# A hybrid decoder layer on one core: the mixer's recurrence, taps and norm put in a fixed order, and the first stage's small changes

## The chip, the cores and the metric

One core of a Trainium2 chip runs the whole layer in one launch. The metric is device time in microseconds (us), the median of several executions. PE is TensorE's matmul, PEld its weight load, DVE VectorE, ACT ScalarE, POOL GpSimd, SP SyncE (which issues most transfers).

## The reference, cut to what matters

The layer works on 512 tokens of 1024 channels in float32. Two half-step feed-forward parts stand around a mixer; each part begins with an RMS norm.

```
x = x + 1/2 * FFN1(rmsnorm(x));  x = x + mixer(rmsnorm(x));  x = x + 1/2 * FFN2(rmsnorm(x));  y = rmsnorm(x)

z = h @ w_in                                   # 4 x 512 channels: c_val, c_gate, r_x, r_gate
u  = c_val * sigmoid(c_gate)
u  = silu(layernorm(depthwise_conv31(u)))      # the convolution's half
xr = depthwise_conv4(r_x)
r, i = sigmoid(blockdiag(xr, w_a)), sigmoid(blockdiag(xr, w_x))      # the two gates
a  = exp(-8 r softplus(-lam));  h_t = a_t h_(t-1) + sqrt(1 - a_t^2) (i_t xr_t)
yr = h * gelu(r_gate)                          # the recurrence's half
mixer = [u ; yr] @ w_out
```

## The kernel before, in words

Every float32 product is made of three products of two parts each, high times high, high times low and low times high. The parts are made on the chip: ACT rounds a tile to its high part, DVE subtracts that from the tile for the low part. In the feed-forward parts a block scheme of seven products is used (`mm_block`, L331); the mixer uses plain products over eight slices of the contraction (`mm_feat`, L316) and products by token tile (`mm_tok`, L557 to L559).

A Python list of `Unit`s is the order of PE's work. For each unit `run` traces its products, then lets generators (`chains`, `convs`, `pool_convs`) trace a step of the side work, and then traces the unit's evacuation. A planner afterwards orders the instructions of each engine by priority, which is the place where they were traced (moved by `tc.high_priority(offset)`), and by its own idea of when each is ready. `tc.keep_in_program_order(ins)`, called `pin` in places, ties an instruction behind the one that was traced just before it on its engine.

In the mixer the units come in this order: the convolution's gate and value for its four channel tiles of 128 (`zc_units`, tiles 0 and 1, then 2), the four tiles of the recurrence's input (`rx_units`), the convolution's tile 3, the four tiles of the recurrence's gate branch (`rg_units`), and the output products (`out_units`). The output products of the recurrence's half read `yhi` and `ylo` (four tiles c, in two pairs q); those of the convolution's half read `uhi` and `ulo`. Token tiles t are 0 to 3, output halves `oh` 0 and 1.

The side work: `conv_dve` makes a convolution tile on DVE, 31 multiply-adds (taps, L704 to L710) into two PSUM banks `pc` and one last addition (L714); tile 1 goes by ACT and POOL (`conv_pool`). `lru` is the recurrence: eight gate products `pga` on PE (L827), a sigmoid on ACT behind each (L828), two products on POOL (L833), tanh, exp and square on ACT (L837 to L842), one product for each pair on DVE (L845), square roots on ACT (L849), products on POOL (L850), then for each pair two scans over time (L859), the product with the GeLU branch `gl` (L864), the high part on ACT (L865) and the low part on DVE (L866). `layernorm` takes the mean by `channel_sum` on PE (`pm`, L677), subtracts it, squares, sums on PE again, takes the root on ACT (L750), the reciprocal on DVE (L763, in two halves of 256 tokens), then product (L767), SiLU (L768), high part (L769) and low part (L759).

In the first stage PE runs products of a constant tile (`keep_busy`, L954, counts in `IDLE`) between the first steps; `grow` is the first norm's weight row, spread over the partitions by two products with one row (L959).

Of the kernel before, what the change touches and what calls it, by code (L numbers as in the profile page):

```python
# [8 lines left out]
F32 = mybir.dt.float32  # L9
# [18 lines left out]
PLAIN = (3, 2)  # L28
BESIDE = (4, 5, 6, 9, 11, 13, 15, 18, 20)
ASIDE = 16  # L30
IDLE = (7, 3, 3, 3)
CUT = 128
TAPS = 31
PR_NORM = 800
# [4 lines left out]
PR_SIDE = -400  # L39
PR_OUT = 300  # L40
PR_COMB = 0
SCAN_LATER = 5
RMS_EPS = 1e-6
LN_EPS = 1e-5
A, B, ALL = (0, HT), (HT, HT), (0, T)
# [30 lines left out]
def layer_kernel(ctx: ExitStack, tc, x, gains, w_g1, w_u1, w_d1a, w_d1b, w_in,  # L76
# [47 lines left out]

    nc.sync.dma_start(xt[0], x[0:P, :])
    grow = sp.tile([1, D], F32, name="grow", tag="gbc", bufs=1)
    nc.sync.dma_start(grow, gains[0:1, :])
    nc.sync.dma_start(xt[1], x[P:2 * P, :])

    def load_gain(i):  # L130
# [9 lines left out]
    def dve(us):  # L140
        clock["dve"] = max(clock["dve"], clock["pe"] - 3.0) + us

    def step_chains():
        for c in list(chains):
            with tc.high_priority(offset=c[0]):
                if next(c[1], None) is None:
                    chains.remove(c)

    def step_convs():
        while convs and clock["dve"] < clock["pe"]:  # L150
            with tc.high_priority(offset=PR_CONV):
                us = next(convs[0], None)
            if us is None:
                convs.pop(0)
            else:
                dve(us)
        while pool_convs and clock["pool"] < clock["pe"]:
            clock["pool"] = max(clock["pool"], clock["pe"] - 3.0)
            with tc.high_priority(offset=PR_CONV):
                us = next(pool_convs[0], None)  # L160
            if us is None:
                pool_convs.pop(0)
            else:
                clock["pool"] += us
# [468 lines left out]
    def par(c, i):  # L633
        return ch[:, c, i:i + 1]

    def zc_units(c, parts):
        off = ASIDE if len(parts) == 2 else 0
        sgt, sv = Slab(split=ws_in[4 + c], off=off), Slab(split=ws_in[c], off=off)
        box = {}

        def product(key, s, t0, n):
            box[key] = bank("pz")
            mm_feat(box[key][:, :n], s, t0, n, CUT if key == "g" and c == 0 else 0)

        def gate_out(n):
            box["s"] = sp.tile([P, T], F32, name=nm("sgc"), tag="sg", bufs=2)
            S.activation(box["s"][:, :n], box["g"][:, :n], AF.Sigmoid)

        def val_out(t0, n):
            V.tensor_mul(mx["ub"][:, c, 30 + t0:30 + t0 + n], box["v"][:, :n], box["s"][:, :n])  # L650
            dve(0.7)
            if c != 1:
                convs.append(conv_dve(c, t0, n))
            elif t0 + n == T:
                pool_convs.append(conv_pool(c))
            if c == 3:
                chains.append((PR_LRU, lru()))

        out_ = []
        for t0, n in parts:  # L660
            us = 5.44 * n / 512
            out_.append(Unit([sgt], us, lambda t0=t0, n=n: product("g", sgt, t0, n),
                             lambda n=n: gate_out(n)))
            out_.append(Unit([sv], us, lambda t0=t0, n=n: product("v", sv, t0, n),
                             lambda t0=t0, n=n: val_out(t0, n)))
        return out_
# [14 lines left out]
    def conv_done(c):  # L681
        done["conv", c] = True
        if c < 3 and all(("conv", i) in done for i in range(3)):
            pm["s"] = slot([P, T], "cs")
            G.tensor_add(pm["s"], conv_out(0), conv_out(2))
            G.tensor_add(pm["s"], pm["s"], conv_out(1))
# [9 lines left out]
    def conv_dve(c, t0, n):  # L696
        if t0 == 0:
            accs[c] = [bank("pc"), bank("pc")]
        acc, o, at = accs[c], conv_out(c), slice(t0, t0 + n)
        us = 0.66 if n == T else 0.42  # L700
        for j in range(TAPS):
            src, to = mx["ub"][:, c, t0 + j:t0 + j + n], acc[j % 2][:, at]
            if j == 0:
                V.tensor_scalar(out=to, in0=src, scalar1=par(c, P_DW),  # L704
                                scalar2=par(c, P_DWB), op0=ALU.mult, op1=ALU.add)
            elif j == 1:
                V.tensor_scalar(out=to, in0=src, scalar1=par(c, P_DW + 1), scalar2=None,
                                op0=ALU.mult)
            else:
                V.scalar_tensor_tensor(out=o[:, at] if j == TAPS - 2 else to, in0=src,  # L710
                                       scalar=par(c, P_DW + j), in1=to,
                                       op0=ALU.mult, op1=ALU.add)
            yield us
        V.tensor_add(o[:, at], acc[0][:, at], o[:, at])  # L714
        yield us
        if t0 + n == T:
            conv_done(c)


    def conv_pool(c):  # L720
# [18 lines left out]
    def layernorm():  # L739
        mu = pm["mean"]  # L740
        sq = [slot([P, 2, T], "sq") for _ in range(2)]
        for c in range(4):
            v = conv_out(c)
            V.tensor_sub(v, v, mu)
            dve(0.69)
            S.activation(sq[c // 2][:, c % 2, :], v, AF.Square)
        yield 1
        var = channel_sum([sq[c // 2][:, c % 2, :] for c in range(4)])
        rs = sp.tile([P, T], F32, name=nm("rs"), tag="sg", bufs=2)
        S.activation(rs, var, AF.Sqrt, bias=lneps)  # L750
        done["var"] = True
        yield 1
        hi, lo = two("uhi", F32R), two("ulo", F32R)
        half = [slice(0, HT), slice(HT, T)]

        def low(sl):
            for c in range(4):
                v, o = conv_out(c)[:, sl], hi[c // 2][:, c % 2, sl]
                V.tensor_sub(lo[c // 2][:, c % 2, sl], v, o.bitcast(F32))  # L759
            dve(1.6)  # L760

        for i, sl in enumerate(half):
            V.reciprocal(rs[:, sl], rs[:, sl])  # L763
            dve(1.8)
            for c in range(4):
                v, o = conv_out(c)[:, sl], hi[c // 2][:, c % 2, sl]
                V.tensor_mul(v, v, rs[:, sl])  # L767
                S.activation(v, v, AF.Silu, scale=par(c, P_LNG), bias=par(c, P_LNB))  # L768
                S.copy(o, v)  # L769
            dve(1.6)  # L770
            if i:
                low(half[0])
        low(half[1])
        done["u"] = (hi, lo)

    lr = {}
# [41 lines left out]
            out_.append(Unit([s], 5.44, lambda c=c, s=s: product(c, s), lambda c=c: evac(c)))  # L818
        return out_

    def lru():
        xr, r, i_, th = lr["xr"], two("r"), two("i"), two("th")
        for c in range(4):
            at = (slice(None), c % 2, slice(None))
            for gi, (to, b) in enumerate(((r, P_BA), (i_, P_BX))):
                pga = bank("pga")
                PE.matmul(pga, bd[:, gi, c, :], xr[c // 2][at], start=True, stop=True)  # L827
                S.activation(to[c // 2][at], pga, AF.Sigmoid, bias=par(c, b))  # L828
            if c % 2:
                yield 1  # L830
        pin = tc.keep_in_program_order
        for q in range(2):
            G.tensor_mul(xr[q], xr[q], i_[q])  # L833
            clock["pool"] += 2.4
# [5 lines left out]
            pin(S.activation(r[c // 2][at], r[c // 2][at], AF.Exp, scale=nsp[:, c:c + 1]))  # L840
        for q in range(2):
            pin(S.activation(i_[q], r[q], AF.Square))  # L842
        yield 1
        for q in range(2):
            pin(V.scalar_tensor_tensor(out=th[q], in0=i_[q], scalar=1.0, in1=th[q],  # L845
                                       op0=ALU.add, op1=ALU.mult))
            dve(1.2)
        for q in range(2):
            S.activation(th[q], th[q], AF.Sqrt)  # L849
            G.tensor_mul(xr[q], xr[q], th[q])  # L850
            clock["pool"] += 2.4
        done["roots"] = True
        for _ in range(SCAN_LATER):
            yield 1
        hi, lo = two("yhi", F32R), two("ylo", F32R)
        for q in range(2):
            for c in (2 * q, 2 * q + 1):
                at = (slice(None), c % 2, slice(None))
                pin(V.tensor_tensor_scan(th[c // 2][at], r[c // 2][at], xr[c // 2][at],  # L859
                                         0.0, ALU.mult, ALU.add))  # L860
                dve(1.2)
            while ("gl", 2 * q + 1) not in done:
                yield 1
            pin(V.tensor_mul(th[q], th[q], lr["gl"][q]))  # L864
            S.copy(hi[q], th[q])  # L865
            V.tensor_sub(lo[q], th[q], hi[q].bitcast(F32))  # L866
            dve(2.4)
            done["y", q] = (hi, lo)


    def out_units(after):
# [31 lines left out]
        def fin_two():  # L903
            for t in range(2):
# [1 line left out]
                    fin(t, oh)  # L906

        out_ = [Unit(sy, 5.44, lambda: part((0, 1), sy, ("y", 0), True, (0, 1))),
                Unit(sy, 2.72, lambda: part((0,), sy, ("y", 1), True, (2, 3))),
                Unit([], 0.0, mean),  # L910
                Unit(sy, 2.72, lambda: part((1,), sy, ("y", 1), True, (2, 3)))]
        out_ += [Unit(sy, 2.72, lambda oh=oh: part((2,), sy, ("y", 1), True, halves=(oh,)))
                 for oh in range(2)]
        out_ += [Unit([], 0.0, lambda: need("var"))]
# [204 lines left out]
    norm_scale(0, xs[0], g1ps)  # L1119
    norm_scale(1, xs[1], g1ps)  # L1120
    pts = []
    for t in range(2):
        pts.append(transposed(t, xs[t]))
        keep_busy(IDLE[2 + t])
        pin(slab_hi(firsts[t]))
    xs2 = [norm_stats(t) for t in (2, 3)]
    for p in pts:
        transposed_lo(p)
# [62 lines left out]
```

## Time and profile before

| what | us |
|---|---|
| median of 3 runs (lowest, highest) | 851.02 (850.5, 852.06) |
| the profiled execution, own time | 851.07 |
| its span in the profile | 849.2 |
| PE busy | 833.4 |
| DVE, ACT, POOL busy | 640.5, 425.0, 91.3 |

The span runs from the first to the last instruction of the profile; 1.87 us of the execution's own time lie outside it. Starts are counted from the span's start. A row of the timeline gives start, busy time, engine, line, operation, output and inputs, shapes, how many instructions were merged into it, and in brackets the engine's idle time before it with what ended that. A matmul's record is longer than its start-to-start distance, since matmuls are pipelined.

### The profile page before, as it was taken

What the parts mean: (1) busy time and instruction counts of PE and PEld (TensorE: products, weight loads), DVE (VectorE), ACT (ScalarE), POOL (GpSimd) and SP (SyncE); (2) the same over time, 40 slices, a digit from 0 to 9 for tenths busy, and PEclk for the clock granted to TensorE, in tenths of its full rate; (3) what the DMA queues carried; (4) which work ended last, traced back from release to release, by engine and by line L of the source; (5) the groups of instructions that cost most, each with busy time, mean ns of one, the idle gap of its engine ahead of it and who ended that gap; (6) DMA issues with size and microseconds to landing.
All of it is one profiled execution on the core that took longest, in us unless ns stands there. A gap on an engine that the chain in (4) does not pass through costs nothing.

```text
span 849.2 us, 13877 instructions
## 1 busy us (share of the span) xinstructions
PE 833.4 (98%) x5608; PEld 759.6 (89%) x5608; DVE 640.5 (75%) x931; ACT 425.0 (50%) x677; POOL 91.3 (11%) x114
## 2 busy tenths in 40 slices
PE   8999999999999999999996999999999999999996
PEld 7999989999889998998875789999889998899985
DVE  5989668998658984598977679896548985558844
ACT  7656534666425662335391755555226554136623
POOL 2001110000110001209740010000000000000001
PEclk9999999999999999999998999999999999999998
DMA  7447895555985579655541032334312334223302
GB/s 266 172 149 261 310 324 198 195 176 174 313 329 182 193 242 375 226 203 194 198 140 59 0 100 70 101 104 150 123 45 86 120 123 152 74 76 100 124 26 100
DMA packets 36722, 139.14 MB, mean 164 GB/s; under 512 B 5041, under 2 KB 5169, under 8 KB 33970
## 3 DMA queue, kind: packets, MB, share of 16 engines
q1 hardware_dynamic: 29170, 112.04, 38.9%
q0 software_dynamic: 6912, 25.17, 7.7%
q8 instruction: 44, 0.72, 0.3%
q10 hardware_dynamic: 576, 1.05, 0.3%
q14 instruction: 20, 0.16, 0.1%
HBM read 110.98 MB, written 27.26 MB: 163 GB/s over the span
## 4 chain that ended last, share of the span: by engine, by line
PE 94%; DVE 2%; ACT 1%; DMA 1%; SPq 0%; issue 0%; POOLq 0%; POOL 0%; ACTq 0%
PE px L331 25%; PE pz L331 12%; PE pz L316 8%; PE pd L557 8%; PE pd L558 8%; PE pd L559 8%; PE pw L331 6%; PE pgate L316 3%; PE pup L316 3%; PE po L557 2%; PE po L559 2%; PE po L558 2%; PE pdl L559 1%; PE pdl L557 1%; PE pdl L558 1%; DMA xt<-in_x 1%
## 5 line engine op out<-in xcount | busy, mean ns | idle before, releaser
L215 DVE TENSOR_TENSOR hl<-raw,hl 128x1024 fp32r<-128x1024 f32 (+1 forms) x132 | 139.8, 1061 | 40.3 <-ACT hl L206 26.8
L215 DVE TENSOR_TENSOR hl<-tt,hl 128x1024 fp32r<-128x1024 f32 x78 | 94.9, 1216 | 34.8 <-ACT hl L242 21.1
L331 PE MATMUL px<-sx,hl 128*128 128x256 f32 x936 | 118.8, 276 | 0.0
L331 PE MATMUL pz<-sx,hl 128*128 128x256 f32 x936 | 118.8, 276 | 0.0
L557 PE MATMUL pd<-hl,act 128*128 128x512 f32 x304 | 118.6, 390 | 0.0
L558 PE MATMUL pd<-hl,act 128*128 128x512 f32 x304 | 118.4, 389 | 0.0
L559 PE MATMUL pd<-hl,act 128*128 128x512 f32 x304 | 118.3, 389 | 0.0
L331 PEld LDWEIGHTS pz<-sx,hl 128*128 128x128 f32 x936 | 111.9, 188 | 0.0
L331 PEld LDWEIGHTS px<-sx,hl 128*128 128x128 f32 x936 | 111.9, 188 | 0.0
L331 PE MATMUL px<-h_hi,hl 128*128 128x256 f32 x630 | 96.9, 277 | 0.0
L242 ACT CAST hl<-tt 128x1024 fp32r<-128x1024 f32 x78 | 81.8, 1051 | 26.4 <-PE pd L559 20.3
L331 PEld LDWEIGHTS px<-h_hi,hl 128*128 128x128 f32 x630 | 83.7, 188 | 1.4 <-DVE um L529 0.7
L242 ACT CAST hl<-raw 128x1024 fp32r<-128x1024 f32 x78 | 65.1, 835 | 38.9 <-PE pd L559 26.3
L206 ACT CAST hl<-raw 128x1024 fp32r<-128x1024 f32 x54 | 56.1, 1051 | 46.5 <-PE pd L559 39.7
L559 PEld LDWEIGHTS pd<-hl,act 128*128 128x128 f32 x304 | 57.1, 188 | 11.9
L557 PEld LDWEIGHTS pd<-hl,act 128*128 128x128 f32 x304 | 57.1, 188 | 11.5
L558 PEld LDWEIGHTS pd<-hl,act 128*128 128x128 f32 x304 | 57.1, 188 | 11.4
L316 PE MATMUL pz<-h_hi,hl 128*128 128x512 f32 (+2 forms) x322 | 63.0, 346 | 0.0
L710 DVE SCALAR_TENSOR_TENSOR pc<-sx,ch,pc 128x256 f32<-128x256 f32 (+1 forms) x112 | 61.4, 615 | 0.1
L316 PEld LDWEIGHTS pz<-h_hi,hl 128*128 128x128 f32 x322 | 51.7, 188 | 7.9 <-issue 0.5
L300 DVE TENSOR_TENSOR slo<-sraw,shi 128x1024 fp32r<-128x1024 f32 x24 | 29.3, 1219 | 28.0 <-ACT shi L299 28.0
L331 PE MATMUL px<-h_lo,hl 128*128 128x256 f32 x312 | 48.2, 277 | 0.0
(186 smaller groups left out, 1317.1 us busy)
## 6 DMA issues: line engine op xcount, KB each, us to landing
raw<-in_w_g SPq DMA_DIRECT2D x44, 512.0 KB, 3.5
raw<-in_w_u SPq DMA_DIRECT2D x44, 512.0 KB, 4.4
hl<-wsi SPq DMA_DIRECT2D x16, 1024.0 KB, 4.8
sraw<-in_w_in SPq DMA_DIRECT2D x16, 512.0 KB, 6.4
wsi<-shi POOLq DMA_DIRECT2D x16, 512.0 KB, 5.2
wsi<-slo POOLq DMA_DIRECT2D x16, 512.0 KB, 5.5
raw<-in_w_d1a SPq DMA_DIRECT2D x16, 512.0 KB, 4.7
raw<-in_w_d2a SPq DMA_DIRECT2D x16, 512.0 KB, 3.5
```

The lines of the kernel that those rows point to most:

```text
L206: return S.copy(s.hi, s.raw)
L215: ins = V.tensor_sub(s.lo, s.raw, s.hi.bitcast(F32))
L242: S.copy(s.hi, s.raw)
L300: V.tensor_sub(lo, raws[-1], hi.bitcast(F32))
L316: ins = PE.matmul(ps[:, c0:c1], w[:, k, :], h[:, k, t0 + c0:t0 + c1], start=(i == 0 and k == 0), stop=(i == 2 and k == KT - 1))
L331: PE.matmul(ps[:, c0:c1], w[:, k * P:(k + 1) * P], h[:, k, c0:c1], start=(first and i == 0 and k == 0), stop=(i == 2 and k == 3), skip_gro ...
L557: PE.matmul(ps, ahi, whi, start=first, stop=False)
L558: PE.matmul(ps, ahi, wlo, start=False, stop=False)
L559: PE.matmul(ps, alo, whi, start=False, stop=last)
L710: V.scalar_tensor_tensor(out=o[:, at] if j == TAPS - 2 else to, in0=src, scalar=par(c, P_DW + j), in1=to, op0=ALU.mult, op1=ALU.add)
```

## The change

- **Recurrence and taps.** When convolution tile 3 is evacuated, all taps still outstanding of the other tiles are traced, then the recurrence at once: its eight gate products (now ahead of the first `rg` unit's products, no longer behind them), sigmoids and what follows, all tied. Tile 3's taps are handed to `lru`, which places them by hand: 17 ahead of L845, 4 ahead of the first scan, 1 ahead of the first pair's GeLU product, 2 ahead of each pair's low part, the rest behind the second pair. `SCAN_LATER`, which held the scans back for five steps, is gone.
- **Output products.** The mean's products stand behind both token tiles of the second pair, no longer between them.
- **Norm.** A tied SiLU of a 16-column tile follows the root; the reciprocal's second half comes behind the first half's products; all is tied in an order written out.
- **Convolution's gate.** Its sigmoid is traced with a raised priority.
- **First stage.** Idle products 11, 1, 1, 2 for 7, 3, 3, 3; `grow` comes by ACT's queue; the first weight tile's high part stands ahead of the first transposes' copies on ACT.

```diff
-IDLE = (7, 3, 3, 3)
+IDLE = (11, 1, 1, 2)
-SCAN_LATER = 5
...
-    nc.sync.dma_start(grow, gains[0:1, :])
+    nc.scalar.dma_start(grow, gains[0:1, :])
...
+    def step_conv():
+        with tc.high_priority(offset=PR_CONV):
+            us = next(convs[0], None)
+        if us is None:
+            convs.pop(0)
+        else:
+            dve(us)
...
-            S.activation(box["s"][:, :n], box["g"][:, :n], AF.Sigmoid)
+            with tc.high_priority(offset=PR_OUT):
+                S.activation(box["s"][:, :n], box["g"][:, :n], AF.Sigmoid)
...
-            if c != 1:
+            if c == 3:
+                while convs:
+                    step_conv()
+                chains.append((PR_LRU, lru(conv_dve(c, t0, n))))
+                step_chains()
+            elif c != 1:
                 convs.append(conv_dve(c, t0, n))
...
-            if c == 3:
-                chains.append((PR_LRU, lru()))
...
+            if c == 3:
+                tc.keep_in_program_order(ins)
             yield us
...
-        S.activation(rs, var, AF.Sqrt, bias=lneps)
+        tc.keep_in_program_order(S.activation(rs, var, AF.Sqrt, bias=lneps))
+
+        junk = sp.tile([P, 16], F32, name=nm("ss"), tag="ss", bufs=4)
+        tc.keep_in_program_order(S.activation(junk, ones[:, 0:16], AF.Silu))
...
+        def high(sl):
+            for c in range(4):
+                v, o = conv_out(c)[:, sl], hi[c // 2][:, c % 2, sl]
+                pin(V.tensor_mul(v, v, rs[:, sl]))
+                pin(S.activation(v, v, AF.Silu, scale=par(c, P_LNG), bias=par(c, P_LNB)))
+                pin(S.copy(o, v))
...
+        def low(sl, cs):
+            for c in cs:
                 v, o = conv_out(c)[:, sl], hi[c // 2][:, c % 2, sl]
+                pin(V.tensor_sub(lo[c // 2][:, c % 2, sl], v, o.bitcast(F32)))
...
+        h0, h1 = slice(0, HT), slice(HT, T)
+        pin(V.reciprocal(rs[:, h0], rs[:, h0]))
+        high(h0)
+        low(h0, (0,))
+        pin(V.reciprocal(rs[:, h1], rs[:, h1]))
+        low(h0, (1, 2, 3))
+        high(h1)
+        low(h1, range(4))
...
-    def lru():
+
+    def lru(conv):
+        def taps(n):
+            for us in (next(conv, None) for _ in range(n)):
+                dve(us or 0.0)
...
-                S.activation(to[c // 2][at], pga, AF.Sigmoid, bias=par(c, b))
-            if c % 2:
-                yield 1
-        pin = tc.keep_in_program_order
+                pin(S.activation(to[c // 2][at], pga, AF.Sigmoid, bias=par(c, b)))
...
-        yield 1
+        taps(17)
...
-            S.activation(th[q], th[q], AF.Sqrt)
+            pin(S.activation(th[q], th[q], AF.Sqrt))
...
-        for _ in range(SCAN_LATER):
-            yield 1
...
+            taps(0 if q else 4)
...
+            taps(0 if q else 1)
             pin(V.tensor_mul(th[q], th[q], lr["gl"][q]))
-            S.copy(hi[q], th[q])
-            V.tensor_sub(lo[q], th[q], hi[q].bitcast(F32))
+            pin(S.copy(hi[q], th[q]))
+            taps(2)
+            pin(V.tensor_sub(lo[q], th[q], hi[q].bitcast(F32)))
...
+        taps(TAPS)
+        yield 1
...
-                Unit(sy, 2.72, lambda: part((0,), sy, ("y", 1), True, (2, 3))),
-                Unit([], 0.0, mean),
-                Unit(sy, 2.72, lambda: part((1,), sy, ("y", 1), True, (2, 3)))]
+                Unit(sy, 5.44, lambda: part((0, 1), sy, ("y", 1), True, (2, 3))),
+                Unit([], 0.0, mean)]
...
+    pin(slab_hi(firsts[0]))
     for t in range(2):
         pts.append(transposed(t, xs[t]))
         keep_busy(IDLE[2 + t])
-        pin(slab_hi(firsts[t]))
+    pin(slab_hi(firsts[1]))
```

## Rows read from the trace of the kernel before

**Rows 1.** The page, its span and busy time.
```profile
span 849.2 us, 13877 instructions
...
PE 833.4 (98%) x5608; PEld 759.6 (89%) x5608; DVE 640.5 (75%) x931; ACT 425.0 (50%) x677; POOL 91.3 (11%) x114
```

**Rows 2.** PE's waits: total us, times, longest.
```profile
PE po L557 <- ACT yhi L865: 6.4, 1, 6.4
```

**Rows 3.** Windows around the wait: length, busy of PE, PEld, DVE, ACT, POOL, then granted clock.
```profile
450.00:453.93 3.93, 0.00 (x0) 0.00 (x1) 3.89 (x5) 1.10 (x2) 0.00 (x0) 0.75 0.38 161
...
456.00:457.00 1.00, 1.00 (x4) 0.78 (x3) 1.00 (x2) 0.00 (x0) 0.00 (x0) 0.50 0.00 0
```

**Rows 4.** Timeline of the mixer's recurrence, from its gate products to the output products.
```profile
422.89 0.81 DVE L704 TENSOR_SCALAR pc<-sx,ch 128x512 f32<-128x512 f32 x1
...
424.11 7.03 PE L827 MATMUL pga<-xr,bd 128*128 128x512 f32 x16
...
427.61 0.75 DVE L707 TENSOR_SCALAR pc<-sx,ch 128x512 f32<-128x512 f32 x1 [0.74 <-ACT r L828]
...
438.10 2.00 ACT L842 ACTIVATE i<-r 128x1024 f32<-128x1024 f32 x2
...
439.17 2.36 DVE L845 SCALAR_TENSOR_TENSOR th<-i,th 128x1024 f32<-128x1024 f32 x2 [3.58 <-ACT i L842]
...
441.40 2.01 ACT L849 ACTIVATE th<-th 128x1024 f32<-128x1024 f32 x2
441.45 7.33 DVE L710 SCALAR_TENSOR_TENSOR pc<-sx,ch,pc 128x512 f32<-128x512 f32 x11
442.61 4.77 POOL L850 TENSOR_TENSOR xr<-xr,th 128x1024 f32<-128x1024 f32 x2 [8.26 <-ACT th L849]
...
445.51 1.97 PE L316 MATMUL pz<-h_hi,hl 128*128 128x512 f32 x8
448.70 2.33 DVE L859 TENSOR_TENSOR_SCAN th<-r,xr 128x512 f32<-128x512 f32 x2
...
451.58 1.22 DVE L864 TENSOR_TENSOR th<-th,gl 128x1024 f32<-128x1024 f32 x1
...
452.83 1.04 ACT L865 CAST yhi<-th 128x1024 fp32r<-128x1024 f32 x1 [6.53 <-DVE th L864]
...
453.93 0.80 PE L557 MATMUL po<-hl,yhi 128*128 128x512 f32 x1 [6.45 <-ACT yhi L865]
...
454.17 1.22 DVE L866 TENSOR_TENSOR ylo<-th,yhi 128x1024 fp32r<-128x1024 f32 x1
...
458.91 0.39 PE L559 MATMUL po<-hl,ylo 128*128 128x512 f32 x1
```

**Rows 5.** Timeline of the norm over channels, to the first product that reads it.
```profile
464.62 1.02 PE L677 MATMUL pm<-cs,ones 128*128 128x512 f32 x2
...
473.69 3.37 DVE L763 RECIPROCAL rs<-rs 128x256 f32<-128x256 f32 x2 [4.67 <-ACT rs L750]
...
477.40 1.28 ACT L768 ACT_TABLE_LOAD   x1 [3.74 <-DVE cv L767]
...
480.12 0.76 DVE L759 TENSOR_TENSOR ulo<-cv,uhi 128x256 fp32r<-128x256 f32 x2 [0.44 <-ACT uhi L769]
...
483.44 0.39 PE L557 MATMUL po<-hl,uhi 128*128 128x512 f32 x1
```

**Rows 6.** Timeline of the first stage.
```profile
1.04 3.36 PE L954 MATMUL idle<-warm 128*128 128x128 f32 x14 [1.04 <-DVE warm L946]
...
1.17 0.32 SPq L127 DMA_DIRECT2D grow<-in_gains  x1
...
8.98 1.05 ACT L206 CAST hl<-raw 128x1024 fp32r<-128x1024 f32 x1
...
18.45 1.22 PE L316 MATMUL pgate<-h_hi,hl 128*128 128x256 f32 x8 [1.11 <-ACT hl L206]
```

**Rows 7.** The chain that ended last, its first stage: start, us, what.
```profile
5.23 10.03 DMA xt<-in_x
```

More of the change, by code (lines that the diff above doesn't have):

```diff
@@ L147, in step_chains @@
                     chains.remove(c)
+    def step_conv():
[5 more added lines that the diff above has]
+            dve(us)
     def step_convs():
         while convs and clock["dve"] < clock["pe"]:
[L151 to L156, printed above, removed]
+            step_conv()
         while pool_convs and clock["pool"] < clock["pe"]:
@@ L651, in val_out @@
             dve(0.7)
-            if c != 1:
+            if c == 3:
+                while convs:
+                    step_conv()
+                chains.append((PR_LRU, lru(conv_dve(c, t0, n))))
+                step_chains()
+            elif c != 1:
                 convs.append(conv_dve(c, t0, n))
@@ L703, in conv_dve @@
             if j == 0:
-                V.tensor_scalar(out=to, in0=src, scalar1=par(c, P_DW),
-                                scalar2=par(c, P_DWB), op0=ALU.mult, op1=ALU.add)
+                ins = V.tensor_scalar(out=to, in0=src, scalar1=par(c, P_DW),
+                                      scalar2=par(c, P_DWB), op0=ALU.mult, op1=ALU.add)
             elif j == 1:
-                V.tensor_scalar(out=to, in0=src, scalar1=par(c, P_DW + 1), scalar2=None,
-                                op0=ALU.mult)
-            else:
-                V.scalar_tensor_tensor(out=o[:, at] if j == TAPS - 2 else to, in0=src,
-                                       scalar=par(c, P_DW + j), in1=to,
-                                       op0=ALU.mult, op1=ALU.add)
+                ins = V.tensor_scalar(out=to, in0=src, scalar1=par(c, P_DW + 1),
+                                      scalar2=None, op0=ALU.mult)
+            else:
+                ins = V.scalar_tensor_tensor(out=o[:, at] if j == TAPS - 2 else to, in0=src,
+                                             scalar=par(c, P_DW + j), in1=to,
+                                             op0=ALU.mult, op1=ALU.add)
+            if c == 3:
+                tc.keep_in_program_order(ins)
             yield us
-        V.tensor_add(o[:, at], acc[0][:, at], o[:, at])
-        yield us
+        ins = V.tensor_add(o[:, at], acc[0][:, at], o[:, at])
+        if c == 3:
+            tc.keep_in_program_order(ins)
         if t0 + n == T:
             conv_done(c)
+        yield us
     def conv_pool(c):
@@ L753, in layernorm @@
         hi, lo = two("uhi", F32R), two("ulo", F32R)
-        half = [slice(0, HT), slice(HT, T)]
-        def low(sl):
+        pin = tc.keep_in_program_order
+        def high(sl):
             for c in range(4):
                 v, o = conv_out(c)[:, sl], hi[c // 2][:, c % 2, sl]
-                V.tensor_sub(lo[c // 2][:, c % 2, sl], v, o.bitcast(F32))
+                pin(V.tensor_mul(v, v, rs[:, sl]))
+                pin(S.activation(v, v, AF.Silu, scale=par(c, P_LNG), bias=par(c, P_LNB)))
+                pin(S.copy(o, v))
             dve(1.6)
[L762 to L765, printed above, removed]
+        def low(sl, cs):
+            for c in cs:
                 v, o = conv_out(c)[:, sl], hi[c // 2][:, c % 2, sl]
[L767 to L773, printed above, removed]
+                pin(V.tensor_sub(lo[c // 2][:, c % 2, sl], v, o.bitcast(F32)))
+                dve(0.4)
+        h0, h1 = slice(0, HT), slice(HT, T)
[6 more added lines that the diff above has]
+        low(h1, range(4))
         done["u"] = (hi, lo)
@@ L819, in rg_units @@
         return out_
-    def lru():
+    def lru(conv):
+        def taps(n):
+            for us in (next(conv, None) for _ in range(n)):
+                dve(us or 0.0)
+        pin = tc.keep_in_program_order
         xr, r, i_, th = lr["xr"], two("r"), two("i"), two("th")
```

## The prediction

> **What bounds the kernel now.** I read the page first: PE is busy for 833.4 of the 849.2 us [rows 1], so a change can only return PE's idle time, or time in which PE works slowly. The list of PE's waits comes next. One wait stands out: the first output product `po` waited 6.4 us, in one piece, for the high part `yhi` of the recurrence [rows 2]; the next longest is 1.11 us, in the first stage [rows 6]. [...] Last, the timeline gives the price. The eight products before the wait took 1.97 us with a record of 0.39, so they started (1.97 - 0.39) / 7 = 0.226 us apart, and PE could have started `po` at 445.51 + 8 x 0.226 = 447.32. It started at 453.93: 6.61 us lost (the wait list counts 6.45 from the modelled end of the last product). From there 11 products started before 458.91, in 4.98 us where 11 x 0.226 = 2.49 would have done: 2.49 us more [rows 4]. **This place costs 9.10 us**, and that is all that can be had here.
>
> What came last before the wait ended: the gate products ran from 424.11, behind a whole `rg` unit; the squares ended at 440.10, DVE made `th` at 439.17 after standing idle for 3.58 us, then did 11 taps (441.45 to 448.70) before the first scan, although POOL had the first pair's input ready after 2.4 of its 4.77 us from 442.61, at 445.0 [rows 4]. So there are two delays: the gates come late, and the taps stand in front of the scans.
>
> **The recurrence after the change.** A unit of 24 products is 24 x 0.226 = 5.42 us, so the gate products move from 424.11 to 418.69; PE's total stays, and `rg` still ends at 447.32. Following the chain with the durations of [rows 4]:
> - Squares: 5.42 us earlier, the first at 433.75 (439.17 less 5.42), the second at 434.68.
> - DVE reaches tile 3's taps at 422.89 as before. The 17 ahead of `th` took 439.17 - 3.58 - 422.89 = 12.70 us, of which 0.74 was a wait for a sigmoid to free a PSUM bank. Without it they end at 434.85. Now DVE, not ACT, decides when `th` starts; the pair takes 441.45 - 439.17 = 2.28, to 437.13.
> - Roots: 441.40 - 440.10 = 1.30 after the squares, and after the first half of `th` (435.99): 436.1. POOL follows 442.61 - 441.40 = 1.21 later, 437.3, and is through the first pair at 439.7.
> - Four taps at 7.25 / 11 = 0.66: 437.13 to 439.77. First two scans 439.8; 451.58 - 448.70 is two scans and a tap, 2.88, to 442.7; product to high part 1.25, 443.95; high part to PE 1.10, **445.05**. PE needs it at 447.32: 2.3 us to spare.
> - Two taps and the low part (1.22): 446.4. PE reads it with its third product, at 447.77: 1.4 to spare.
> - Second pair: scans (2.22) to 448.6, high part ready at 450.95, low part at 452.3. PE needs them after 24 products, at 452.74 and 453.19: 1.8 and 0.9 to spare.
> - Five taps and the addition, 6 x 0.66, to 456.2; the mean's product now stands after 48 products, at 458.17: 2.0 to spare.
>
> So I take the whole 9.10 us. The smallest cover is 0.9 us on the second low part: each us by which DVE is later than this costs one beyond that.
>
> **Waits that the ties add.** The first scan waits for POOL until 439.7 and all of DVE stands behind it; that is in the sum. The third GeLU is tied behind the first pair's high part, to about 445, so its PSUM bank is held some 3 us longer than its product needs; the output products ask for banks only at 447.32. The first two GeLUs come after the roots (438.1) and a table load (1.30), and each can be no longer than a root of twice the width, 1.0: 441.4, before DVE asks at 442.7. The last one, behind `rg`'s end, is done by 448.5, DVE asks at 448.6: no margin, but a slip there of some tenths is covered by the 0.9.
>
> **The norm.** From the mean's product (464.62) to the first low part (480.88) took 16.26 us, with 18.82 to the first product that reads it (483.44) [rows 5]. With the mean 12 products later, that cover is 483.44 - 453.93 - 2.49 = 27.02 less 10.85 (48 products), 16.2. The second half of the reciprocal (3.37 / 2 = 1.68) and the table load (1.28) leave the chain [rows 5], so it needs 13.3: 2.9 to spare, no gain and no loss. If neither helped it would be 0.1 late. The extra small SiLU runs while DVE does the reciprocal. The raised priority of the sigmoid and the earlier tracing change no sum: PE has no wait over a tenth in that stretch that the list shows.
>
> **The first stage.** What ends PE's 1.11 us wait at 18.45 is a chain from the last token tile, issued at 5.23 and 10.03 us under way [rows 6, 7]. `grow` no longer takes its 0.32 us on SP ahead of that issue, which bounds the gain: 0 (if the transfers themselves are the limit) to 0.32. I take the middle, **0.16**, since the chain holds both issues and a long transfer. [...] On ACT the issue precedes work that waits for the first tile anyway. The idle products: 8 more records of 3.36 / 14 = 0.24 ahead of `grow`'s products are at most 1.92 later; the weight's high part (1.05) ahead of the transposes' copies delays those by at most 1.05 [rows 6]. Both touch the products before 18.45 and are covered by the 1.11 there; I take 0, with +1.9 (1.92 + 1.05 - 1.11) as the other end.
>
> **Sum**, against the profiled execution's own time, 851.07 (the median, 851.02, is the same within 0.05): 851.07 - 6.61 - 2.49 - 0.16 = **841.8 us**. Alone it has a range of 841.0 to 843.5, from the first stage's bounds and the scatter of the three runs.
>
> **Rivals.**
> - *Tile 3's taps still wait for banks.* Their two PSUM banks come from the same eight that the gate products use, and one wait of this kind is in the trace (0.74). At worst the first tap waits for the last sigmoid: last gate product 431.14 - 5.42 = 425.7, and at most 1.0: 426.7, or 3.8 after 422.89. Then the first high part is 1.5 late, its low part 0.9 more, the second low part 0.5 more: 2.9 us of PE waits, **844.7**. Against it: two banks of tile 2's taps fall free just when tile 3's begin. 0.12.
> - *The gates don't come earlier.* The planner orders PE by its own idea of readiness and the gate products aren't tied; if they stay behind an `rg` unit, only the 11 taps become 4. Then the scans start at 445.0 with POOL, `po` at 450.25: waits of 2.9, 0.9 and 0.5, **846.1**, and 848.6 if the clock falls again as in [rows 3]. For it: nothing ties them; against it: their priority comes from the place where they are traced, ahead of `rg`. 0.08.
> - *Slower: the clock falls in the first stage.* [...] Against it: after the mixer's wait the full clock was back within 5 us of work [rows 4]. 0.03.
> - *Gain lost elsewhere*, within 0.2% of before: 0.02.
>
> **Numbers.** The forecast has 0.75. The range 840.5 to 845.5 takes in the first rival and the upper bound of the first stage, and leaves out the other three (0.13). A difference of 0.2% (1.7 us) is about what a measurement of this kernel can tell. Faster: forecast and the first two rivals, less a little for what I haven't seen, 0.92; same 0.04; slower 0.04.
>
> **What would show it.** In the profile after: no wait of `po` for `yhi` over 1 us in PE's list; the granted clock 1.00 in every window from the last `rg` product on; `pga` ahead of the first `rg` products, some 5.4 us earlier; 17, 4, 1 and 2 taps in DVE's timeline in these places; the first product that reads `uhi` 27.0 us after the first `po` and without a wait; PE busy some 2.5 us less. Wrong it would be if `pga` stands where it stood, if `po` waits for `ylo` or the mean for tile 3's convolution, or if the wait near 18 us grows.

## The result, and the profile after

| what | us |
|---|---|
| before, median of 4 runs (lowest, highest) | 850.82 (850.5, 852.06) |
| changed, median of 4 runs (lowest, highest) | 843.15 (842.88, 844.82) |
| ratio, 95% interval | 0.9911 [0.9894, 0.9929] |
| the changed kernel's profiled execution, own time and span | 842.88, 840.9 |

The change makes the kernel 0.9% faster. The forecast was 841.8 with a range of 840.5 to 845.5: the sign and the mechanism held, the size was 1.35 us too good. The profiled execution is 1.08 us above the forecast, and its profile says where they went: two new waits in the mixer cost 1.31 us, and some 0.3 came back ahead of FFN1.

The page of the changed kernel, its span and busy times, to be read against [rows 1]:

```profile
span 840.9 us, 13877 instructions
...
PE 832.1 (99%) x5606; PEld 759.7 (90%) x5606; DVE 642.6 (76%) x931; ACT 426.2 (51%) x678; POOL 92.0 (11%) x114
```

PE's waits in it, the whole list (total us, times, longest; the first is the wait for the constant tile at the start, as before):

```profile
PE idle L975 <- DVE warm L967: 1.0, 1, 1.0
PE po L561 <- DVE ylo L886: 0.8, 2, 0.5
```

The wait of 6.4 us for `yhi` [rows 2] is gone, and so is the one near 18 us [rows 6]. In their place stand two short waits for the low part `ylo`. That the wait near 18 us is gone can't be put down to the first stage's edits: it is missing from `e1_mixer_only` and `e10_pair2_old_first` too, which keep the old first stage. The clock no longer falls here, as windows over the same stretch show (length, busy of PE, PEld, DVE, ACT, POOL, then granted clock), against 0.75 and 0.50 in [rows 3]:

```profile
447.00:450.00 3.00, 2.76 (x12) 1.97 (x11) 3.00 (x3) 0.60 (x1) 0.00 (x0) 1.00 0.64 197
...
453.00:456.00 3.00, 2.48 (x11) 1.75 (x10) 3.00 (x5) 0.00 (x0) 0.00 (x0) 1.00 0.00 0
```

The timeline of the recurrence in the changed kernel, rows of PE, DVE, ACT and POOL together (`pga` L849, POOL's second products L869, scans L877, product L883, high part L884, low part L886, taps L716), to be read against [rows 4]:

```profile
418.15 7.03 PE L849 MATMUL pga<-xr,bd 128*128 128x512 f32 x16
...
433.62 2.36 DVE L864 SCALAR_TENSOR_TENSOR th<-i,th 128x1024 f32<-128x1024 f32 x2
...
435.44 2.01 ACT L868 ACTIVATE th<-th 128x1024 f32<-128x1024 f32 x2
...
436.64 4.76 POOL L869 TENSOR_TENSOR xr<-xr,th 128x1024 f32<-128x1024 f32 x2 [6.69 <-ACT th L868]
...
439.09 4.51 DVE L877 TENSOR_TENSOR_SCAN th<-r,xr 128x512 f32<-128x512 f32 x2 [0.47 <-POOL xr L869]
...
445.40 1.05 ACT L884 CAST yhi<-th 128x1024 fp32r<-128x1024 f32 x1 [5.55 <-DVE th L883]
...
446.61 1.22 DVE L886 TENSOR_TENSOR ylo<-th,yhi 128x1024 fp32r<-128x1024 f32 x1
446.80 0.39 PE L559 MATMUL po<-hl,yhi 128*128 128x512 f32 x1
447.03 0.39 PE L560 MATMUL po<-hl,yhi 128*128 128x512 f32 x1
447.25 0.39 PE L559 MATMUL po<-hl,yhi 128*128 128x512 f32 x1
447.74 2.33 DVE L877 TENSOR_TENSOR_SCAN th<-r,xr 128x512 f32<-128x512 f32 x2
447.88 0.50 PE L561 MATMUL po<-hl,ylo 128*128 128x512 f32 x1 [0.24 <-DVE ylo L886]
448.22 0.39 PE L559 MATMUL po<-hl,yhi 128*128 128x512 f32 x1
...
453.01 0.39 PE L560 MATMUL po<-hl,yhi 128*128 128x512 f32 x1
...
453.91 0.50 PE L561 MATMUL po<-hl,ylo 128*128 128x512 f32 x1 [0.52 <-DVE ylo L886]
454.25 0.39 PE L559 MATMUL po<-hl,yhi 128*128 128x512 f32 x1
```

Read it from the top. The gate products stand 5.96 us earlier (the forecast 5.42, and 0.5 from the first stage), and `th`, the roots and POOL follow as forecast. Then two scans take 4.51 us, while the two of the second pair take 2.33. The views of the single instructions at 439 us show that it is the first scan alone, and that POOL's product for the second pair began 0.09 us before it:

```profile
439.00 2.40 POOL L869 TENSOR_TENSOR xr<-xr,th 128x1024 f32<-128x1024 f32 x1
439.09 3.39 DVE L877 TENSOR_TENSOR_SCAN th<-r,xr 128x512 f32<-128x512 f32 x1 [0.47 <-POOL xr L869]
```

It took 3.39 us, where the median of the four is 1.21, and it ended at 442.48, 1.08 us after POOL's product for the second pair (436.64 + 4.76 = 441.40). What is late by this reaches PE as the two waits for `ylo`: 448.22 - 447.25 = 0.97 and 454.25 - 453.01 = 1.24 from start to start over two products, where 2 x 0.227 is the pitch, so 0.52 + 0.79 = 1.31 us (PE's list, which counts from the modelled ends, has 0.8).

How the gain is spread over the span is read from the first product of three stages. In the timeline of PE, FFN1's first `px`, the mixer's first `pz` and FFN2's first `px`, before:

```profile
47.82 0.74 PE L331 MATMUL px<-h_hi,hl 128*128 128x256 f32 x5
...
351.12 1.21 PE L316 MATMUL pz<-h_hi,hl 128*128 128x256 f32 x9
...
531.13 0.73 PE L331 MATMUL px<-h_hi,hl 128*128 128x256 f32 x5
```

and after:

```profile
47.33 0.74 PE L333 MATMUL px<-h_hi,hl 128*128 128x256 f32 x5
...
350.60 1.21 PE L318 MATMUL pz<-h_hi,hl 128*128 128x256 f32 x9
...
522.83 0.73 PE L333 MATMUL px<-h_hi,hl 128*128 128x256 f32 x5
```

Of the gain, 0.5 us came ahead of FFN1; FFN1 gave nothing, the mixer 180.01 - 172.23 = **7.78 us**, and all that follows nothing. The mixer's own length, from its first `pz` to FFN2's first `px`, is used below, since it repeats to some hundredths while whole runs of one kernel differ by 1 to 3 us: those of the kernel before lie in two groups, at 850.5 to 851.3 and at 852.1 to 853.6 us.

### The profile page after: what moved, and what is told of

It is laid out like the page before. It is cut to its first block, busy times and chain, and to the rows that moved or that the text cites. A ratio compares the mean times of both kernels' runs of the same rounds, so it can differ in the third digit from the quotient of the medians.

```text
span 840.9 us, 13877 instructions
## 1 busy us (share of the span) xinstructions
PE 832.1 (99%) x5606; PEld 759.7 (90%) x5606; DVE 642.6 (76%) x931; ACT 426.2 (51%) x678; POOL 92.0 (11%) x114
## 4 chain that ended last, share of the span: by engine, by line
PE 96%; DVE 2%; ACT 1%; issue 0%; POOL 0%; POOLq 0%; DVEq 0%; ACTq 0%
PE px L333 25%; PE pz L333 13%; PE pd L560 8%; PE pd L559 8%; PE pd L561 8%; PE pz L318 8%; PE pw L333 6%; PE pgate L318 3%; PE pup L318 3%; PE po L561 2%; PE po L559 1%; PE po L560 1%; PE ptr L371 1%; PE pdl L561 1%; PE pdl L560 1%; PE pdl L559 1%
## 5 line engine op out<-in xcount | busy, mean ns | idle before, releaser
L716 DVE SCALAR_TENSOR_TENSOR pc<-sx,ch,pc 128x256 f32<-128x256 f32 (+1 forms) x112 | 61.3, 617 | 0.0
L301 ACT CAST shi<-sraw 128x1024 fp32r<-128x1024 f32 x24 | 25.3, 1053 | 47.7 <-DMA sraw<-in_w_out 23.3
```

The costliest lines, as they stand in the source:

```text
L301: S.copy(hi, raws[-1])
L716: ins = V.scalar_tensor_tensor(out=o[:, at] if j == TAPS - 2 else to, in0=src, scalar=par(c, P_DW + j), in1=to, op0=ALU.mult, op1=ALU.add)
```

## The experiments

The theory: GpSimd's second product, running beside the first scan, holds DVE for some 2.2 us, and that uses up the margins of the low parts. Its rivals: the scan is slow for another reason; or the missing 1.3 us are lost elsewhere (first stage, norm, taps). Ratios are to the kernel before, run beside each group of experiments on the same chip.

**The second pair's product on VectorE** (`e5_pair2_dve`, and once more beside the changed kernel):

```diff
             pin(S.activation(th[q], th[q], AF.Sqrt))
-            G.tensor_mul(xr[q], xr[q], th[q])
+            if q == 0:
+                G.tensor_mul(xr[q], xr[q], th[q])
...
             taps(0 if q else 4)
+            if q:
+                pin(V.tensor_mul(xr[q], xr[q], th[q]))
```

> The changed kernel with the second pair's product of input and root on VectorE, ahead of the second pair's scans, instead of on GpSimd. Theory: the first scan took 3.4 us because GpSimd was at work on that product beside it; without it both scans take 1.2 each, the first low part comes about 2.2 us earlier and costs PE no wait, the second about 1 us earlier (VectorE takes on 1.2 us) and costs 0.3 us at most; gain 1.0 to 1.3 us over the changed kernel, about 842.0. Rival (the scan waits for data or is slow in its first call): the first scan takes 3.4 us again, the second low part is 1.2 us later than now and the time is about 844.4.

> The changed kernel as it is, beside the next kernels on one chip. Expected 843.0 us, 0.991 of the kernel before; its first scan again near 3.4 us, with GpSimd's second product beside it.

> The version with the second pair's product on VectorE once more, beside the changed kernel on the same chip. If GpSimd's second product beside the first scan is what cost the changed kernel its waits for the low parts, this is 1.3 us below the changed kernel (about 841.6), and all four scans take 1.2 us. If the difference seen before was one of chips, the two are equal within 0.5 us.

Measured: 841.44 us (841.16 to 841.61), 0.9876 [0.986, 0.9892]. Run once more, beside the changed kernel: 842.57 (841.45 to 843.66), 0.9883 [0.9867, 0.99], beside 843.06 (842.1 to 843.94), 0.9889 [0.9874, 0.9904] for the changed kernel, whose first two scans took 4.51 us again. DVE's and POOL's timeline of the first of these:

```profile
436.87 2.40 POOL L870 TENSOR_TENSOR xr<-xr,th 128x1024 f32<-128x1024 f32 x1 [6.70 <-ACT th L868]
...
439.31 2.34 DVE L881 TENSOR_TENSOR_SCAN th<-r,xr 128x512 f32<-128x512 f32 x2 [0.46 <-POOL xr L870]
...
445.80 1.22 DVE L877 TENSOR_TENSOR xr<-xr,th 128x1024 f32<-128x1024 f32 x1
447.05 2.34 DVE L881 TENSOR_TENSOR_SCAN th<-r,xr 128x512 f32<-128x512 f32 x2
...
451.95 1.22 DVE L890 TENSOR_TENSOR ylo<-th,yhi 128x1024 fp32r<-128x1024 f32 x1
```

All four scans take 1.20 to 1.23 us, the product costs DVE 1.22, and PE's list has no wait of `po` at all. The mixer's length is 170.87 in both profiles of this version and 172.23 and 172.22 in both of the changed kernel: 1.36 us less, which is nearly the 1.31 of the two waits. By the mixer's length the theory holds, on one chip too, so the difference is not one of chips. The whole time expected of the repeat missed: the medians are 0.49 us apart, not 1.3, and the ratios do not tell the two kernels apart, since whole runs scatter by more than this.

**Eleven taps ahead of the first scan** (`e7_taps_11`): `taps(0 if q else 11)` for 4.

> The changed kernel with 11 taps ahead of the first scan, as before the change, instead of 4. Theory: the scan starts 4.6 us later than with 4 taps, at 443.7, when GpSimd is done, so it takes 1.2 us and not 3.4; first high part 2.4 us later than now, PE waits about 1.9 us for it and in all 2 to 3 us, about 844.5. Rival (the scan is slow whatever runs beside it): it takes 3.4 us here too, PE waits 4 to 5 us, about 847.

Measured: 844.48 us, 0.9914 [0.99, 0.9928]; mixer 174.05, 1.82 us longer than the changed kernel's. Its DVE and POOL in the timeline:

```profile
436.20 7.33 DVE L716 SCALAR_TENSOR_TENSOR pc<-sx,ch,pc 128x512 f32<-128x512 f32 x11
436.95 4.76 POOL L869 TENSOR_TENSOR xr<-xr,th 128x1024 f32<-128x1024 f32 x2 [6.70 <-ACT th L868]
...
443.44 2.33 DVE L877 TENSOR_TENSOR_SCAN th<-r,xr 128x512 f32<-128x512 f32 x2
```

The scans begin after POOL has ended (441.7) and take 1.2 us each, a second proof of the cause. The 11 taps that now run beside POOL's products take 7.33 us. A single tap's record is 0.75, so they start (7.33 - 0.75) / 10 = 0.66 us apart. The 11 taps of [rows 4], which also take 7.33, are no comparison, as they too ran beside POOL (442.61 to 447.38). Three taps of the changed kernel that ran with POOL idle are one:

```profile
453.77 2.07 DVE L716 SCALAR_TENSOR_TENSOR pc<-sx,ch,pc 128x512 f32<-128x512 f32 x3
```

They start (2.07 - 0.75) / 2 = 0.66 us apart as well: it is the scan that POOL disturbs, not the tap. Seven taps more cost far less than their 4.6 us (7 x 0.66), since 2.2 of them fill time that the scan would have lost.

**One input instead of two on GpSimd** (`e11_pool_one_input`):

```diff
-            G.tensor_mul(xr[q], xr[q], th[q])
+            if q:
+                G.tensor_scalar(out=xr[q], in0=th[q], scalar1=0.5, scalar2=None, op0=ALU.mult)
+            else:
+                G.tensor_mul(xr[q], xr[q], th[q])
```

> The changed kernel with GpSimd's second product replaced by a scaling of one input (half of the root, so the input's part of the second pair's recurrence is left out). If the first scan stands still for as long as GpSimd works on memory beside it, whatever the number of GpSimd's inputs, the scan again ends 1.2 us after GpSimd's second instruction does, and its record is that instruction's remaining time and 1.2 us. If only two inputs on both sides disturb each other, the scan takes 1.2 us beside it.

Measured: 841.4 us in one run. The instructions at 439 and 441 us:

```profile
438.84 2.82 POOL L870 TENSOR_SCALAR xr<-th 128x1024 f32<-128x1024 f32 x1
438.91 2.07 DVE L880 TENSOR_TENSOR_SCAN th<-r,xr 128x512 f32<-128x512 f32 x1 [0.47 <-POOL xr L872]
440.90 1.19 DVE L880 TENSOR_TENSOR_SCAN th<-r,xr 128x512 f32<-128x512 f32 x1
```

Both expectations miss: the scan is longer by 0.87 us, not by the whole 2.8 and not by nothing, and it ends 0.68 us before POOL does. By this one run, how much longer the scan takes depends on what POOL runs (0.87 us beside the scaling, 2.18 beside the product); why it is 0.87 here stays open.

**The gates left behind the first `rg` unit** (`e6_gates_behind`): without the `step_chains()` that starts the recurrence when tile 3 is evacuated.

> The changed kernel with the recurrence's eight gate products traced behind the first unit of the gate branch, as before the change; taps, scans, norm and first stage as changed. Theory: squares and th come 5.4 us later, the first scan cannot start before about 444.5, and PE waits some 4 to 6 us in all (the scan is slowed here too); about 848 us, up to 850 if the clock falls in the wait. Rival (the taps in front of the scans were the whole delay): no more than 1 us over the changed kernel, 844.

Measured: 848.98 us (848.26 to 850.84), 0.9968 [0.9955, 0.998]. PE's waits:

```profile
PE po L559 <- ACT yhi L883: 5.0, 1, 5.0
```

and the timeline of its first output products:

```profile
452.84 0.80 PE L559 MATMUL po<-hl,yhi 128*128 128x512 f32 x1 [4.98 <-ACT yhi L883]
453.44 0.63 PE L560 MATMUL po<-hl,yhi 128*128 128x512 f32 x1
```

and a window behind them:

```profile
454.00:455.00 1.00, 1.00 (x4) 0.69 (x3) 1.00 (x2) 0.00 (x0) 0.00 (x0) 0.50 0.00 0
```

The wait is back, and so is the lower clock level: records of 0.63 us at a granted clock of 0.50. Of the mixer's 7.78 us only 1.27 are left (its length is 178.74): the earlier gates carry the gain, the moved taps little without them. The first scan takes 3.40 us here too.

**The norm's code of before** (`e8_norm_before`): `layernorm` as it was, from the root to the last low part; the mean's place as changed.

> The changed kernel with the norm over channels as before the change (no early SiLU, no ties, both halves of the reciprocal first); the mean's product stays where the change puts it. Theory: the cover of 16.2 us against 16.3 needed leaves a wait of 0 to 0.3 us at the first product that reads the norm, time within 0.4 us of the changed kernel, 843.1 to 843.5. Rival (the norm's new order carries part of the gain): a wait of more than 1 us there, 844.2 or more.

Measured: 843.32 us, 0.9909 [0.9892, 0.9926]; no wait for `uhi` or `ulo`; mixer 172.27 against 172.23. The norm's edits give and cost nothing here.

**The first stage.** Four kernels: the mixer's edits alone; the first stage's edits alone; the row's queue alone in the kernel before; and the version of `e5_pair2_dve` with the first stage of before. A fifth keeps the longer idle rows (`IDLE = (11, 3, 3, 3)`).

```diff
-IDLE = (11, 1, 1, 2)
+IDLE = (7, 3, 3, 3)
...
-    nc.scalar.dma_start(grow, gains[0:1, :])
+    nc.sync.dma_start(grow, gains[0:1, :])
...
-    pin(slab_hi(firsts[0]))
     for t in range(2):
         pts.append(transposed(t, xs[t]))
         keep_busy(IDLE[2 + t])
-    pin(slab_hi(firsts[1]))
+        pin(slab_hi(firsts[t]))
```

> The changed kernel with the first stage of before (idle products 7, 3, 3, 3, the weight row by SyncE, the old order of the first high part). Theory: nearly all of the gain is the mixer's, 7.8 us, so about 843.2 us, with the granted clock 1.00 from 6 to 14 us and the 1.1 us wait near 18 us back. Rival: the first stage's stretch at half speed costs more than its earlier transfers bring, then this version is faster than the changed kernel, about 842.

> The kernel before with the first stage of the changed one alone. Theory: 0.5 us faster than before, about 850.3, the last token tile's square on ScalarE near 14.1 us (before 15.35), the granted clock 0.50 for some 3 us after 9.5 us, the mixer's wait of 6.4 us unchanged. Rival (the two effects cancel): 850.8, and the feed-forward products from 40 us on at the same times as before.

> The kernel before with the weight row's transfer on ScalarE's queue and nothing else. Theory: the row's small transfer in SyncE's queue holds back those behind it by more than its 0.32 us of issue; the last token tile's square starts about 1.2 us earlier, near 14.1, and the kernel gains about 1 us, 849.8. Rival (issue time is all): the square starts 0.3 us earlier, the kernel gains at most 0.3 us, 850.5.

> The changed kernel with idle products 11, 3, 3, 3 in place of 11, 1, 1, 2. Theory: the clock fell at 9.5 us because PE had less to do between the transposes; with the old counts it stays at 1.00, the first products start about 0.5 us earlier and the kernel is 0.3 to 1.0 us faster than the changed one, about 842.4. Rival: the fall comes with the longer row ahead of the weight row's products, not with the short ones; then the clock falls here too and the time stays within 0.3 us of 843.1.

> The same version with the first stage of the kernel before (idle products 7, 3, 3, 3, the row by SyncE's queue, the old order of the first high parts). If the first stage's edits give what their earlier transfers promise, it is about 1 us slower than the version with them; if, as the earlier runs suggest, they are worth no more than 0.5 us, it is between 841.4 and 842.2 us, not to be told from it.

Measured (`px` is FFN1's first, third token tile's square on ACT, granted clock as the mean of 8 to 14 us):

| kernel | median us | ratio, 95% | square | clock | `px` |
|---|---|---|---|---|---|
| mixer's edits alone (`e1_mixer_only`) | 845.29 | 0.9915 [0.9901, 0.9928] | 13.42 | 0.72 | 47.77 |
| first stage's edits alone (`e2_first_only`) | 851.9 | 0.9993 [0.9981, 1.0004] | 12.64 | 0.77 | 46.45 |
| the row's queue alone (`e3_row_only`) | 852.46 | 0.9999 [0.9989, 1.001] | 15.63 | 1.00 | 49.75 |
| long idle rows (`e4_idle_kept`) | 843.02 | 0.9892 [0.9879, 0.9906] | 13.63 | 0.74 | 47.78 |
| product on VectorE, old first stage (`e10_pair2_old_first`) | 843.97 | 0.9893 [0.9876, 0.9909] | 15.47 | 1.00 | 49.93 |
| before | 851.07 (profiled) | | 13.99 | 1.00 | 47.82 |
| changed | 842.88 (profiled) | | 13.02 | 0.72 | 47.33 |

No ratio shows an effect of the first stage by itself: 0.9993 holds 1, and the ratios of kernels run side by side with and without it overlap (0.9892, with the long idle rows, and 0.9915; 0.9883 for the second run of `e5_pair2_dve`'s version and 0.9893). But the medians all lean to the new stage, by 0.8, 2.3 and 1.4 us, so a gain of this order is neither shown nor ruled out. The last of these is the first outcome that was expected of `e10_pair2_old_first` (about 1 us slower); its 843.97 lies outside the 841.4 to 842.2 of the other. The profiles hint at a small effect: in the nine with all its edits (the changed kernel twice, and seven experiments) `px` starts at 46.38 to 47.45, in the three with the old stage at 47.77, 47.82 and 49.93. Each is of one execution, though, and those of `e3_row_only` and `e10_pair2_old_first` are the slowest of their kernel's runs, that of `e1_mixer_only` its fastest. Moving the row alone shows no gain; in its profile the third tile's square came later, not earlier, so the expectation missed. So did that of `e1_mixer_only` on the clock (1.00) and on the wait near 18 us, which did not come back, and the theory of `e4_idle_kept`: the long idle rows don't prevent the fall of the clock. The mixer's length in the last version is 170.88, as with the new first stage: the first stage does not act on the mixer.

## Why the prediction was right, and where it was off

- **What the place costs, 9.10 us.** Right. The mixer gave 7.78 us and the two new waits hold 1.31, in sum 9.09; without those waits (`e5_pair2_dve`) it gave 180.01 - 170.87 = 9.14. The clock stayed at 1.00, so the 2.49 us for the slow products came back with the wait.
- **The chain up to the first scan.** Right to some tenths. With PE 0.52 us earlier all through the mixer, the forecast times become 434.3 for `th`, 435.6 for the roots, 436.8 for POOL and 439.3 for the first scan; they were 433.62, 435.44, 436.64 and 439.09. The taps' bank waits did not come, so the first rival falls. One reading was off: PE reads the first low part with its fourth product (447.88 above), not its third, so the spare there was 1.6 us and not 1.4.
- **The scans: the mis-sized term.** The prediction took 2.22 us for the first pair, from scans that in [rows 4] ran when POOL was idle (its products ended at 447.38, the scans began at 448.70). Moved forward to 439.09, the first ran beside POOL's second product, and the pair took 443.52 - 439.09 = 4.43 to the next instruction (a record of 4.51). The prediction placed POOL's work by when its result is ready ("through the first pair at 439.7") and left out what it does next. In the same count of time the first high part was forecast for 445.05 - 0.52 = 444.53 and was ready for PE at 445.40 + 1.10 = 446.50, 1.97 us later. That left 0.3 us of its 2.3 to spare, but it is more than the spare of the two low parts. That `po` waited for `ylo` is one of the signs that the prediction itself named for being wrong. The time stayed in the range all the same, partly by luck: the range's room was meant for the bank waits and the first stage, not for a scan.
- **"Each us by which DVE is later than this costs one beyond that."** Right as a rule: 1.97 less the smallest cover of 0.9 is 1.1, and the waits are 1.31. With the scans' true length, 2.21 us more for the pair, the sum gives 2.21 - 0.9 = 1.3 us of waits, 843.1.
- **The output products, the mean and the norm.** Right: from the first `po` to the first product that reads `uhi` 475.13 - 446.80 = 28.33 us, which is the forecast 27.0 and the 1.31 of waits; no wait for the mean or `uhi`. The first low part was written by 471.9, 3.2 us ahead, where 2.9 were forecast. That the norm's edits don't matter is shown by `e8_norm_before`.
- **The first stage, 0.16.** Neither its sign nor its size is shown. `px` came 0.5 us earlier in this pair of profiles; between any profile with the new stage and any with the old one the difference is 0.32 to 3.55 us, and the ratios leave 0 open. PE was busy for 18.96 of the first 20 us, where it had been for 17.60, which is why its total fell by 1.3 us and not by the 2.5 forecast. The bound of 0.32 was worked out for the row's place on SP alone; the third tile's square came 0.97 us earlier (13.02 for 13.99), more than that bound. `e3_row_only`, at 0.9999, shows no gain from the row's move, but its interval is about 0.9 us to either side and cannot tell 0 from 0.32. So the earlier transfers come from the edits together or from the scatter between executions, which can't be told from these runs.
- **The slower rival.** Its event came, and the kernel was not slower: the clock did fall to 0.50 in the first stage (below), but for some 3 us. At 0.50 products started 4.98 / 11 = 0.453 us apart instead of 0.226 [rows 3, 4]; if the pace follows the clock so in the first stage too, a mean of 0.72 from 8 to 14 us costs 6 x 0.28 = 1.7 us of PE's work, an estimate, against a forecast gain of 9.3. The fall came with long idle rows too (0.74), and with the old stage (0.72).
- **The gates don't come earlier.** `e6_gates_behind` made this rival: 848.98 us, where 848.6 with the clock's fall was worked out, and 1.27 us of the mixer's gain. That the two figures are so near is partly luck, since the first scan's 3.40 us were not in that sum.

## What to carry to other kernels

A duration from the trace holds for the company in which it was measured: when an instruction is moved, look up what the other engines run at its new place, as GpSimd's product beside the scan here (3.39 us for 1.21). Before pulling a chain forward, list the margins of everything that is late next, and ask what one instruction of unforeseen length does to the smallest. If an engine that frees another one is then in its way, give the work back: here 1.22 us on VectorE were cheaper than 2.4 on GpSimd.

## What the runs showed of the hardware

**A scan took 2.18 us longer beside GpSimd's product.** Beside GpSimd's two-input product (2.40 us) a scan took 3.39 us instead of 1.21, and 3.40 in `e6_gates_behind`; where GpSimd was idle, in `e5_pair2_dve` and `e7_taps_11`, each took 1.20 to 1.23; GpSimd's product was not slowed (2395 to 2408 ns). Taps were not slowed (0.66 us apart beside it and without it). The first scan began 0.09 us after the product and ended 1.08 us after the product's end; the pair ended 2.20 us after it, in `e6_gates_behind` 2.20 and in `e9_changed_again` 2.19. Applied to the forecast, where POOL's second product ends at 437.3 + 4.77 = 442.07, the 1.08 put the first scan's end at 443.15 instead of 439.8 + 2.22 / 2 = 440.91, and 2.24 - 0.9 = 1.3 us of waits would have given about 843.1 at once, by estimate. GpSimd's scaling of one input, 2.82 us long, made the scan longer by 0.87 only, and the scan ended before it. Why a scan takes longer there and a tap does not is not shown.

**The clock fell in the first stage while PE's records show work.** Windows of the changed kernel (columns as above):

```profile
8.00:9.00 1.00, 1.00 (x8) 0.78 (x8) 1.00 (x3) 0.08 (x1) 0.00 (x0) 1.00 1.00 406
9.00:10.00 1.00, 1.00 (x8) 1.00 (x9) 1.00 (x2) 0.94 (x2) 0.00 (x0) 0.75 1.03 422
10.00:11.00 1.00, 1.00 (x7) 1.00 (x6) 1.00 (x3) 0.41 (x2) 0.00 (x0) 0.50 1.02 418
```

and of the version with GpSimd's one input, whose first stage is the same:

```profile
9.00:10.00 1.00, 1.00 (x9) 0.81 (x8) 1.00 (x3) 0.70 (x2) 0.00 (x0) 1.00 1.05 430
10.00:11.00 1.00, 1.00 (x10) 0.77 (x9) 1.00 (x3) 0.93 (x2) 0.00 (x0) 1.00 1.03 422
```

From 9 to 11 us the granted clock is 0.75 and 0.50 in the first kernel and 1.00 in the second. The fall stands in 8 of the 9 profiles with the changed first stage, in the one with long idle rows, and in one of the four with the idle counts of before. What decides it stays open. It costs little as far as one profile can show: without the fall `px` starts at 46.90, between the 46.38 and 47.45 of those with it.
